# Scores and value sums of four heads per group, B's statistics from one sum, x in halves, and a gate on GpSimd's queue, in a two-layer hybrid trunk

## The chip, the cores and the metric

The kernel runs on one core of a Trainium2 chip. The metric is device time in microseconds (us) of one execution, the median of the runs; lower is better. TensorE (PE) multiplies matrices, VectorE (DVE), ScalarE (ACT) and GpSimd (POOL) work on tiles, SyncE (SP) issues most of the transfers. "Product" below means one matmul instruction.

## The reference, cut to what matters

Two layers over 256 tokens of width 2048, all in float32:

```
for l in range(DEPTH):
    h = rms_norm(x, norm_w[l])
    p = h @ w_in[l]                                   # 2048 x 6668
    oa = sliding_window_sink_attention(qa, ka, va, sinks[l]) * silu(za)   # A: 12 heads of 64, window 128
    ob = conformer_conv_module(ub, ...) * silu(zb)    # B: conv over 31 steps, layer norm, 512 x 512
    oc = rms_norm(gated_deltanet(...)) * silu(zc)     # C: 6 heads of 128, delta rule in chunks
    x = x + concatenate([oa, ob, oc]) @ w_out[l]      # 2048 x 2048
```

In A the scores of a head are a product of 64 rows by 128 queries and 128 or 256 keys; after the softmax the weights are transposed and multiplied with the values of 64 columns. In B the mean and the variance over 512 channels (four tiles of 128 channels) are sums over partitions, made on PE with a matrix of 1/512.

## The kernel before, in words

**Precision.** The large products run with both operands split into a high and a low part (`wh`, `wl` of the weights, the two halves of `xhl` of the activations): high by high, high by low, low by high, three products for one. The small products of A, B and C are plain float32.

**The stream of weights.** `Stream.load` has SP bring the weights in stages of up to 1 MB into `st` (three buffers). `Stream.cuts` cuts a stage into granules of 1024 columns in all: ACT rounds a granule to `wh`, then DVE subtracts to get `wl` (three buffers of each). `token_block` multiplies a block of 512 or 268 columns with the activations stationary; `channel_block` takes 256 columns with the weights stationary. The blocks stand in the list `ORDER`; the first is 512 columns of A's queries (`qk`, 96 products of 512 columns).

**The start.** `load_x` brings x in pieces `xc`; `first_x(i)` transposes 256 columns of it on PE (`xtp`, four transposes), DVE copies the result to `xt`, `set_x` makes `xhl` from it (ACT the high part, DVE the low part), `keep_x` writes `xt` to a scratch tensor `xscr` in memory, from which the residual is read back near the layer's end. `squares` sums the squares of x on ACT; from these come `msq`, on POOL `rstd`, and on PE the row `rowp` of the norm's scale, without which no block's sum can be scaled and leave its PSUM bank. `late_loads` has POOL issue 18 transfers of small parameters (`crow`, `alog`, `prow`, `snk`, `posi`, ...). The masks (`mean_b`, `ucum`, `amask`) come from POOL too.

**A.** `pair(pr)` takes two heads: four products `sc` into two banks, the softmax on DVE and ACT, six transposes `ptp`, six products `ov`. At most two pairs are under way at a time (`"pair": 2`).

**B.** `mixer_b` runs 30 taps of the convolution on DVE and ACT; then `mu` (two products), the squares, `bss` (four products), the row `rowp` of 1/std, the scaled and activated `bs`, which `channel_block` multiplies with the pointwise weights (`PWAT = 4`: after four blocks of the output projection).

**The order.** Tasks are Python generators. Every operation is noted by a `Meter` and put out by `Pace`, which holds for each engine a time from which it is free, with costs written into `price`, and always puts out the operation that by these costs can start first; the trunk's large products go ahead of the tasks unless a task's operation fits in. What comes out is one fixed list for each engine, and each engine works through its list in order. So an operation that is noted later but waits for nothing is put ahead of one noted earlier that waits:

```
for key, l in self.open.items():
    if l:
        free, m = self.at[key], margin if key == "P" else 0.0
        t = max(free, min(n.ready for n in l) + m)
        if t < at or t == at and not best:
            best, at = min((n for n in l if n.ready + m <= t), key=lambda n: n.task.rank), t
```

All instructions are recorded under one line (L346, the call in `Pace.emit`), so rows of the profile are told apart by their tiles.

Of the kernel before, what the change touches and what calls it, by code (L numbers as in the profile page):

```python
# [17 lines left out]
P = 128  # L18
# [409 lines left out]
def hybrid_trunk(ctx: ExitStack, tc: tile.TileContext, x, positions, norm_w, w_in, q_norm_w,  # L428
# [56 lines left out]
    xv = x[0].rearrange("(t p) c -> p t c", p=P)  # L485
    xcs, xat, cols_left = [], [], {}

    def load_x(*cols):

        j = len(xat) // 2  # L490
        if len(xcs) == j:
            xcs.append(big([P, 2, 512], "xc"))
# [27 lines left out]
    posi = const.tile([P, 2], I32, name="posi")  # L520
    crow = [big([DEPTH * KC, 9 * P], "crow") for _ in range(2)]
    pace.free["big"] -= 2

    def late_loads():
        cw = c_conv_w.rearrange("l k c -> (l k) c")
# [104 lines left out]
    ready = []  # L630

# [36 lines left out]
    class Stream:  # L668
# [45 lines left out]
        def cuts(self):  # L714
# [3 lines left out]
            for i, (si, kk, cc, end) in enumerate(self.granules):  # L718
# [7 lines left out]
                S.activation(hi, v, AF.Copy)  # L726
                V.tensor_tensor(lo, v, hi.bitcast(F32), ALU.subtract)
# [52 lines left out]
    def token_block(n, step, act):  # L780
        accs = accs_of(2)
        for k0 in range(0, KT, step):
            hi, lo = stream.next()
            for k in range(step):
                a = act(k0 + k)
                for tb in range(2):
                    ts = slice(tb * P, (tb + 1) * P)
                    acc = accs[tb][:, :n]
                    f, e = k0 + k == 0, k0 + k == KT - 1
                    PE.matmul(acc, a[:, 0, ts], hi[:, k, :], start=f, stop=False)  # L790
                    PE.matmul(acc, a[:, 0, ts], lo[:, k, :], start=False, stop=False)
                    PE.matmul(acc, a[:, 1, ts], hi[:, k, :], start=False, stop=e)
        return accs
# [22 lines left out]
    def keep_x(l, i, xt):  # L816

        (G if l else Q).dma_start(xscr[i], xt.rearrange("p a t -> p (a t)"))
# [10 lines left out]
    def squares():  # L829

        for j in range(4):
            yield lambda: len(xat) > 2 * j + 1
            for tb in range(2):
                sq = mid([P, 512], "sq")
                S.activation(sq, xcs[j][:, tb], AF.Square, accum_out=ssx[:, tb, j:j + 1])
# [411 lines left out]
    def mixer_b(l, h, res):  # L1247
# [51 lines left out]
        V.tensor_tensor(sq[:, 0:2, :], sq[:, 0:2, :], sq[:, 2:4, :], ALU.add)  # L1299
        yield 1  # L1300
        ps = bank([P, 2], "bss")
        for tb in range(2):
            for c in range(2):
                PE.matmul(ps[:, tb:tb + 1], sq[:, c, tb * P:(tb + 1) * P], mean_b[:, 0:1],
                          start=(c == 0), stop=(c == 1))
# [372 lines left out]
    def a_first(l, stt, res):  # L1678
# [61 lines left out]
        def pair(pr):  # L1740
            yield {"mx": 2, "pair": 1}
            pss = [bank([P, 384], "sc") for _ in range(2)]
            for cols, to in ((slice(0, P), slice(0, P)), (slice(P, T), slice(P, 384))):
                for r in range(2):
                    rs = slice(64 * r, 64 * r + 64)
                    PE.matmul(pss[r][:, to], qT[rs, pr, cols], kT[rs, (2 * pr + r) // 3, 0:cols.stop],
                              start=True, stop=True)
            yield
            s2 = []
            for r in range(2):  # L1750
                h = 2 * pr + r
                ps = pss[r]
                s = mp.tile([P, 384], F32, tag="as", bufs=4, name=nm("sm"))
                sk = snk[:, l, h:h + 1]
                V.tensor_tensor_reduce(s[:, 0:P], ps[:, 0:P], amask[:, 1, :], 1.0, sk, ALU.add,
                                       ALU.max, mx[:, h, 0:1])
                V.tensor_tensor_reduce(s[:, P:], ps[:, P:], am, 1.0, sk, ALU.add, ALU.max,
                                       mx[:, h, 1:2])
                s2.append(s)
            drop(2)  # L1760
            hs = slice(2 * pr, 2 * pr + 2)
            V.tensor_scalar(nm_[:, hs, :], mx[:, hs, :], -1.0, None, ALU.mult)
            V.tensor_tensor(ex[:, hs, :], nm_[:, hs, :],
                            snk[:, l, hs].unsqueeze(2).to_broadcast([P, 2, 2]), ALU.add)
            yield
            S.activation(ex[:, hs, :], ex[:, hs, :], AF.Exp)
            for r in range(2):
                h = 2 * pr + r
                for b, seg in ((0, slice(0, P)), (1, slice(P, 384))):
                    S.activation(s2[r][:, seg], s2[r][:, seg], AF.Exp, bias=nm_[:, h, b:b + 1],  # L1770
                                 accum_out=den[:, h, b:b + 1])
            yield
            V.tensor_tensor(den[:, hs, :], den[:, hs, :], ex[:, hs, :], ALU.add)
            V.reciprocal(den[:, hs, :], den[:, hs, :])
            yield
            for r in range(2):
                h = 2 * pr + r
                for b, seg in ((0, slice(0, P)), (1, slice(P, 384))):
# [102 lines left out]
```

## Time and profile before

| | |
|---|---|
| median of 3 runs | 910.84 us (910.77 to 911.11) |
| profiled execution | 913.37 us, its span 911.7 us |
| PE busy | 897.4 us of the span |
| DVE, ACT, POOL busy | 727.9, 567.3, 74.2 us |
| granted TensorE clock | 1.00 throughout |

The span runs from the first to the last instruction of the profiled execution. An engine is busy while one of its instructions is under way; products overlap, so the time that a product costs is read from the start of one to the start of the next. In a row of the timeline, the brackets give the idle time ahead of it and what ended it.

### The profile page before, as it was taken

What the parts mean: (1) busy time and instruction counts of PE and PEld (TensorE: products, weight loads), DVE (VectorE), ACT (ScalarE), POOL (GpSimd) and SP (SyncE); (2) the same over time, 40 slices, a digit from 0 to 9 for tenths busy, and PEclk for the clock granted to TensorE, in tenths of its full rate; (3) what the DMA queues carried; (4) which work ended last, traced back from release to release, by engine and by line L of the source; (5) the groups of instructions that cost most, each with busy time, mean ns of one, the idle gap of its engine ahead of it and who ended that gap; (6) DMA issues with size and microseconds to landing.
All of it is one profiled execution on the core that took longest, in us unless ns stands there. A gap on an engine that the chain in (4) does not pass through costs nothing.

```text
span 911.7 us, 15429 instructions
## 1 busy us (share of the span) xinstructions
PE 897.4 (98%) x5856; PEld 791.8 (87%) x5856; DVE 727.9 (80%) x1405; ACT 567.3 (62%) x1092; POOL 74.2 (8%) x93
## 2 busy tenths in 40 slices
PE   6999999999999999999999999999999999999998
PEld 5899888887789888999888988888788988899998
DVE  5855778999999999657765577699999999985553
ACT  5647845668867665546544596457687676645542
POOL 5000032021001000000000000501200010000000
PEclk9999999999999999999999999999999999999999
DMA  9866467544343655757766554865525435665681
GB/s 301 265 190 185 156 191 195 174 127 134 95 155 96 185 185 161 235 196 264 236 200 192 185 186 148 219 185 153 150 60 167 135 115 186 192 216 184 200 271 36
DMA packets 146186, 161.92 MB, mean 178 GB/s; under 512 B 8191, under 2 KB 129649, under 8 KB 146112
## 3 DMA queue, kind: packets, MB, share of 16 engines
q1 hardware_dynamic: 143808, 155.40, 54.0%
q0 software_dynamic: 2256, 5.52, 2.6%
q8 instruction: 46, 0.75, 0.4%
q14 instruction: 28, 0.23, 0.1%
q10 hardware_dynamic: 48, 0.02, 0.0%
HBM read 152.67 MB, written 8.26 MB: 177 GB/s over the span
## 4 chain that ended last, share of the span: by engine, by line
PE 73%; DVE 13%; issue 5%; DMA 4%; ACT 3%; POOL 1%; SPq 0%; DVEq 0%; POOLq 0%; ACTq 0%
PE acc L346 65%; DVE wl L346 4%; DVE bacc L346 4%; DVE z L346 2%; PE ov L346 1%; DMA xc<-in_x_dram 1%; ACT junk L346 1%; DMA sub<-scry 1%; PE gram L346 1%; PE tsum L346 1%; PE sc L346 1%; DMA scrm<-sub 1%; DMA ms<-scrm 1%; PE ptp L346 1%; ACT wh L346 1%
## 5 line engine op out<-in xcount | busy, mean ns | idle before, releaser
L346 PE MATMUL acc<-xhl,wh 128*128 128x512 f32 x1344 | 476.4, 395 | 0.0
L346 DVE TENSOR_TENSOR wl<-st,wh 128x1024 fp32r<-128x1024 f32 (+1 forms) x276 | 337.8, 1224 | 132.1 <-ACT wh L346 129.3
L346 ACT ACTIVATE wh<-st 128x1024 fp32r<-128x1024 f32 (+1 forms) x276 | 292.3, 1059 | 219.4 <-PE acc L346 194.8
L346 PE MATMUL acc<-xhl,wl 128*128 128x256 f32 x1344 | 382.9, 285 | 0.0
L346 PEld LDWEIGHTS acc<-xhl,wh 128*128 128x128 f32 x1344 | 252.8, 188 | 55.4 <-issue 2.7
L346 PEld LDWEIGHTS acc<-xhl,wl 128*128 128x128 f32 x1344 | 253.4, 189 | 5.6 <-issue 4.7
L346 PE MATMUL acc<-wh,xhl 128*128 128x512 f32 (+1 forms) x384 | 108.0, 365 | 2.7 <-ACT wh L346 2.7
L346 PEld LDWEIGHTS acc<-wh,xhl 128*128 128x128 f32 x384 | 68.6, 191 | 13.7 <-ACT wh L346 3.1
L346 PE MATMUL acc<-wl,xhl 128*128 128x512 f32 (+1 forms) x192 | 69.7, 363 | 0.5 <-DVE wl L346 0.5
L346 DVE SCALAR_TENSOR_TENSOR bacc<-bh,cbt,bacc 128x254 f32<-128x254 f32 (+19 forms) x160 | 68.3, 462 | 0.1
L346 PE MATMUL acc<-yc,wh 128*128 128x256 f32 (+1 forms) x300 | 65.7, 305 | 0.0
L346 PE MATMUL acc<-ya,wh 128*128 128x256 f32 (+1 forms) x300 | 65.5, 305 | 0.0
L346 PE MATMUL acc<-yc,wl 128*128 128x256 f32 x180 | 50.9, 283 | 0.0
L346 PE MATMUL acc<-ya,wl 128*128 128x256 f32 x180 | 50.6, 281 | 0.0
L346 PEld LDWEIGHTS acc<-ya,wh 128*128 128x128 f32 x300 | 48.2, 188 | 2.5
L346 PEld LDWEIGHTS acc<-yc,wh 128*128 128x128 f32 x300 | 48.2, 188 | 2.4
L346 DVE SCALAR_TENSOR_TENSOR ca<-z,cct,ca 128x255 f32<-128x255 f32 (+2 forms) x108 | 47.9, 499 | 2.2 <-ACT ca L346 2.1
L346 ACT ACTIVATE bpr<-bh,cbt 128x255 f32<-128x255 f32 (+9 forms) x80 | 37.6, 488 | 10.1 <-DVE bacc L346 10.0
L346 PE MATMUL acc<-yb,wh 128*128 128x256 f32 (+1 forms) x200 | 43.2, 305 | 0.0
L346 PEld LDWEIGHTS acc<-wl,xhl 128*128 128x128 f32 x192 | 36.6, 191 | 6.4 <-DVE wl L346 1.0
L346 PEld LDWEIGHTS acc<-ya,wl 128*128 128x128 f32 x180 | 34.1, 190 | 0.0
L346 PEld LDWEIGHTS acc<-yc,wl 128*128 128x128 f32 x180 | 34.0, 189 | 0.1
(305 smaller groups left out, 1118.1 us busy)
## 6 DMA issues: line engine op xcount, KB each, us to landing
st<-in_w_in_dram SPq DMA_DIRECT2D x102, 1024.0 KB, 5.3
st<-in_w_out_dram SPq DMA_DIRECT2D x16, 768.0 KB, 5.0
st<-in_w_out_dram SPq DMA_DIRECT2D x10, 1024.0 KB, 5.7
st<-in_w_out_dram SPq DMA_DIRECT2D x12, 512.0 KB, 3.8
st<-in_w_out_dram SPq DMA_DIRECT2D x16, 256.0 KB, 5.6
st<-in_w_in_dram SPq DMA_DIRECT2D x4, 512.0 KB, 8.9
xscr<-xt SPq DMA_DIRECT2D x8, 256.0 KB, 8.7
xt<-xscr SPq DMA_DIRECT2D x8, 256.0 KB, 5.1
```

What stands on the lines that cost most here:

```text
L346: n.f(*n.a, **n.k)
```

## The change

Five things. Two pairs of heads become one task `pairs(p0)`: eight `sc` products into four banks, and twelve `ov` products into one bank with one copy; the two pairs go through the softmax one behind the other. B's two sums over channels get one more addition on DVE, and one product each where there were two. x is loaded and laid out in halves of 256 columns, `set_x` reads the transposes from PSUM and the copy `xt` is made behind it, and the first granule of weights is cut in two pieces. `token_block` multiplies with `wh` first, for both halves of the tokens, and with `wl` last. And a copy on POOL, `gate`, reads the tenth tile of `xhl`; `late_loads` and the layer's first `keep_x` begin when that copy has been noted, and the writes to `xscr` go out from POOL instead of SP.

```diff
-    xv = x[0].rearrange("(t p) c -> p t c", p=P)
+    xv = x[0].rearrange("(t p) (h c) -> p h t c", p=P, c=256)
...
-            a = 256 * (len(xat) % 2)
-            Q.dma_start(xcs[j][:, :, a:a + c], xv[:, :, 512 * j + a:512 * j + a + c])
-            xat.extend(c // 256 * [True])
+            for _ in range(c // 256):
+                h = len(xat) % 2
+                Q.dma_start(xcs[j][:, h], xv[:, 2 * j + h])
+                xat.append(True)
...
+    def hold():
+
+        yield lambda: (0, GATE) in xhl
+        G.tensor_copy(gate, xhl[0, GATE][:, 0, 0:1].bitcast(F32))
+        ready.append("gate")
+        yield "G"
+
     def late_loads():
+        yield lambda: "gate" in ready
...
-                S.activation(hi, v, AF.Copy)
-                V.tensor_tensor(lo, v, hi.bitcast(F32), ALU.subtract)
+                for a in range(0, k, k if i else 1):
+                    b = k if i else a + 1
+                    S.activation(hi[:, a:b], v[:, a:b], AF.Copy)
+                    V.tensor_tensor(lo[:, a:b], v[:, a:b], hi[:, a:b].bitcast(F32), ALU.subtract)
...
-                for tb in range(2):
-                    ts = slice(tb * P, (tb + 1) * P)
-                    acc = accs[tb][:, :n]
-                    f, e = k0 + k == 0, k0 + k == KT - 1
-                    PE.matmul(acc, a[:, 0, ts], hi[:, k, :], start=f, stop=False)
-                    PE.matmul(acc, a[:, 0, ts], lo[:, k, :], start=False, stop=False)
-                    PE.matmul(acc, a[:, 1, ts], hi[:, k, :], start=False, stop=e)
+                f, e = k0 + k == 0, k0 + k == KT - 1
+                for w, part in ((hi, 0), (hi, 1), (lo, 0)):
+                    for tb in range(2):
+                        PE.matmul(accs[tb][:, :n], a[:, part, tb * P:(tb + 1) * P], w[:, k, :],
+                                  start=f and w is hi and not part, stop=e and w is lo)
...
-        (G if l else Q).dma_start(xscr[i], xt.rearrange("p a t -> p (a t)"))
+        G.dma_start(xscr[i], xt.rearrange("p a t -> p (a t)"))
...
         V.tensor_tensor(s2, acc[:, 0:2, :], acc[:, 2:4, :], ALU.add)
+        V.tensor_tensor(s2[:, 0], s2[:, 0], s2[:, 1], ALU.add)
         yield 1
         mu = bank([P, T], "mu")
-        for c in range(2):
-            PE.matmul(mu, mean_b, s2[:, c, :], start=(c == 0), stop=(c == 1))
+        PE.matmul(mu, mean_b, s2[:, 0], start=True, stop=True)
...
-        def pair(pr):
-            yield {"mx": 2, "pair": 1}
-            pss = [bank([P, 384], "sc") for _ in range(2)]
...
+        def pairs(p0):
+
+            both = (p0, p0 + 1)
+            yield {"mx": 4, "pair": 2}
+            pss = [bank([P, 384], "sc") for _ in range(4)]
...
+            op = bank([P, 2, T], "ov")
+            for pr in both:
                 for j in range(3):
-                    PE.transpose(ps[:, j, :], s2[r][:, j * P:(j + 1) * P], ident)
...
+                    for r in range(2):
+                        PE.matmul(op[64 * r:64 * r + 64, pr - p0, P * (j > 0):P * (j > 0) + P],
+                                  va[:, j // 2, (2 * pr + r) // 3, :],
+                                  s2[2 * (pr - p0) + r][:, P * j:P * j + P], start=(j < 2), stop=(j != 1))
...
-        V.tensor_copy(xt, ps)
-        drop()
-        done_x(i // 2)
-        yield
-        yield from set_x(0, i, xt)
+        done_x(i // 2)
+        yield from set_x(0, i, ps)
+        V.tensor_copy(xt, ps)
+        drop()
+        yield
...
         def rest():
+            yield lambda: "gate" in ready
             keep_x(0, i, xt)
```

On POOL, at the start of the program, the changed kernel's list reads as follows (`crow` to `snk` are parameters, `xscr<-xt` the first writes of x).

```order
L346 MEMSET expo 128x64 x2
L346 DMA crow_100<-in_c_conv_w_dram 8x1152
L346 DMA crow_101<-in_c_conv_w_dram 8x1152
L346 DMA alog<-in_c_a_log_dram 128x12
...
L346 DMA prow<-in_k_norm_w_dram 2x48 x2
L346 DMA snk<-in_sinks_dram 128x24
L346 COPY gate<-xhl_256 128x1
L346 DMA posi<-in_positions_dram 128x2x1
L346 DMA xscr<-xt_18_141 128x512
L346 DMA xscr<-xt_28_174 128x512
```

The gate's copy stands behind 17 of the 18 parameter transfers, in the places that they had before; behind it come `posi`, the eight writes of x (before on SP), the masks, and then `rstd`.

On PE, at the start of the program, the changed kernel's list begins so (`acc` are the two sums of the first block, `xtp` sets of four transposes of x).

```order
L346 MATMUL xtp_115<-ident,xc_77 128x128 x4
L346 MATMUL acc_122<-wh_119,xhl_142 128x512
L346 MATMUL acc_123<-wh_119,xhl_142 128x512
L346 MATMUL acc_122<-wh_119,xhl_142 128x512
L346 MATMUL acc_123<-wh_119,xhl_142 128x512
L346 MATMUL xtp_118<-ident,xc_77 128x128 x4
L346 MATMUL acc_122<-wl_120,xhl_142 128x512
L346 MATMUL acc_123<-wl_120,xhl_142 128x512
```

Before, a product with `wl` was the second of the block, and the first five products were followed by twelve transposes at once; now four products with `wh` come first, and the sets of transposes stand between products one or two at a time.

On PE, in A of the first layer, two heads' value sums and the next scores stood like this before (`acc` are products of the input projection).

```order
L346 MATMUL ov_2618<-sm_2378,va_835 64x128
L346 MATMUL acc_2461<-xhl_214,wl_2395 128x256
L346 MATMUL acc_2460<-xhl_270,wh_2462 128x512
L346 MATMUL acc_2460<-xhl_270,wl_2463 128x256
L346 MATMUL acc_2460<-xhl_271,wh_2462 128x512
L346 MATMUL ov_2618<-sm_2379,va_835 64x128
L346 MATMUL ov_2618<-sm_2378,va_835 64x128
L346 MATMUL ov_2618<-sm_2379,va_835 64x128
L346 MATMUL ov_2618<-sm_2378,va_835 64x128
L346 MATMUL ov_2618<-sm_2379,va_835 64x128
```

In the changed kernel four heads' value sums stand like this (`cz` are products of C).

```order
L346 MATMUL ov_2944<-sm_2454,va_842 64x128
L346 MATMUL ov_2944<-sm_2453,va_842 64x128
L346 MATMUL ov_2944<-sm_2454,va_842 64x128
L346 MATMUL ov_2944<-sm_2563,va_842 64x128
L346 MATMUL cz_2923<-cvr_2440,mt_2218 128x128
L346 MATMUL ov_2944<-sm_2564,va_842 64x128
L346 MATMUL ov_2944<-sm_2563,va_842 64x128
L346 MATMUL ov_2944<-sm_2564,va_842 64x128
L346 MATMUL ov_2944<-sm_2563,va_842 64x128
L346 MATMUL ov_2944<-sm_2564,va_842 64x128
```

A pair's six `ov` products were broken one to five by other products, in 11 of the 12 pairs of both layers; now the twelve of four heads are broken once, seven to five, in all six groups. The scores of both layers stood in 15 runs and now stand in 9.

## Rows read from the trace of the kernel before

**Rows 1.** The page, parts 1 and 2: PE's busy time and its clock.

```profile
PE 897.4 (98%) x5856; PEld 791.8 (87%) x5856; DVE 727.9 (80%) x1405; ACT 567.3 (62%) x1092; POOL 74.2 (8%) x93
...
PEclk9999999999999999999999999999999999999999
```

**Rows 2.** Timeline of all engines at the start: start, length, engine, instruction, count.

```profile
5.03 0.69 DVE L346 COPY xt<-xtp 128x512 f32<-128x512 f32 x1 [0.97 <-PE xtp L346]
...
6.57 1.04 ACT L346 ACTIVATE wh<-st 128x1024 fp32r<-128x1024 f32 x1
...
7.66 0.80 PE L346 MATMUL acc<-wh,xhl 128*128 128x512 f32 x1 [2.67 <-ACT wh L346]
...
12.19 2.82 PE L346 MATMUL xtp<-ident,xc 128*128 128x128 f32 x12 [1.20 <-DMA xc<-in_x_dram]
...
15.67 0.63 PE L346 MATMUL acc<-wl,xhl 128*128 128x512 f32 x1
...
16.09 1.05 PE L346 MATMUL acc<-wh,xhl 128*128 128x512 f32 x2
...
17.23 0.63 PE L346 MATMUL acc<-wh,xhl 128*128 128x512 f32 x2
...
18.39 0.40 PE L346 MATMUL acc<-wl,xhl 128*128 128x512 f32 x1
```

**Rows 3.** Stretches at the start: engines' busy time, clock, DMA share, GB/s.

```profile
0.00:5.00 5.00, 1.40 (x5) 0.89 (x5) 0.36 (x2) 1.28 (x1) 4.33 (x15) 1.00 0.56 182
5.00:10.00 5.00, 1.88 (x4) 1.19 (x5) 3.04 (x5) 2.91 (x4) 2.60 (x6) 1.00 1.04 229
10.00:15.00 5.00, 3.80 (x16) 3.08 (x15) 1.84 (x3) 2.11 (x7) 2.72 (x6) 1.00 1.05 364
```

**Rows 4.** Timeline of POOL: its first transfers, and the norm's power.

```profile
1.65 1.25 POOL L346 DMA_DIRECT2D crow<-in_c_conv_w_dram  x2
...
31.09 0.98 POOL L346 TENSOR_TENSOR rstd<-msq,expo 128x2 f32<-128x2 f32 x1 [12.23 <-DVE msq L346]
```

**Rows 5.** Issues that touch xscr: ns min/median/max, first and last start in us.

```profile
L346 SPq DMA_DIRECT2D xscr<-xt x8: 319/658/2007, 10.9 to 28.6; - x8
...
L346 POOL DMA_DIRECT2D xscr<-xt x4: 540/546/609, 418.9 to 464.0; - x4
```

**Rows 6.** Timeline of PE around one pair's value sums in layer 0.

```profile
255.81 0.40 PE L346 MATMUL acc<-xhl,wh 128*128 128x512 f32 x1
256.13 0.43 PE L346 MATMUL ov<-sm,va 128*64 128x128 f32 x2
256.50 0.38 PE L346 MATMUL acc<-xhl,wl 128*128 128x256 f32 x1
256.72 0.39 PE L346 MATMUL acc<-xhl,wh 128*128 128x512 f32 x1
257.04 0.87 PE L346 MATMUL ov<-sm,va 128*64 128x128 f32 x10
257.84 0.38 PE L346 MATMUL acc<-xhl,wl 128*128 128x256 f32 x1
```

**Rows 7.** Timeline of PE around one pair's scores in layer 0.

```profile
242.03 0.93 PE L346 MATMUL sc<-akT,aqT 64*128 64x128 f32 x8
242.88 0.38 PE L346 MATMUL acc<-xhl,wl 128*128 128x256 f32 x1
```

**Rows 8.** Timeline of PE around B's statistics in layer 0.

```profile
361.38 1.10 PE L346 MATMUL mu<-s,mean_b 128*128 128x256 f32 x4 [0.91 <-DVE s L346]
362.13 0.47 PE L346 MATMUL acc<-xhl,wl 128*128 128x256 f32 x1
...
366.40 0.95 PE L346 MATMUL bss<-mean_b,bsq 128*128 128x1 f32 x8
```

**Rows 9.** Timeline of DVE and PE around B's pointwise products in layer 0.

```profile
383.05 0.69 DVE L346 TENSOR_TENSOR bs<-bacc,bs 128x512 fp32r<-128x512 f32 x1
...
400.65 0.40 PE L346 MATMUL acc<-bs,wh 128*128 128x256 f32 x2
```

More of the change, by code (lines that the diff above doesn't have):

```diff
@@ L1302, in mixer_b @@
         for tb in range(2):
-            for c in range(2):
-                PE.matmul(ps[:, tb:tb + 1], sq[:, c, tb * P:(tb + 1) * P], mean_b[:, 0:1],
-                          start=(c == 0), stop=(c == 1))
+            PE.matmul(ps[:, tb:tb + 1], sq[:, 0, tb * P:(tb + 1) * P], mean_b[:, 0:1],
+                      start=True, stop=True)
         yield
@@ L1738, in a_first @@
         left = [HA // 2]
-        def pair(pr):
-            yield {"mx": 2, "pair": 1}
-            pss = [bank([P, 384], "sc") for _ in range(2)]
[L1743 to L1747, printed above, removed]
+        def pairs(p0):
[3 more added lines that the diff above has]
+            for pr in both:
+                for cols, to in ((slice(0, P), slice(0, P)), (slice(P, T), slice(P, 384))):
+                    for r in range(2):
+                        rs = slice(64 * r, 64 * r + 64)
+                        PE.matmul(pss[2 * (pr - p0) + r][:, to], qT[rs, pr, cols],
+                                  kT[rs, (2 * pr + r) // 3, 0:cols.stop], start=True, stop=True)
@@ L1748, in pair @@
             yield
             s2 = []
[L1750 to L1764, printed above, removed]
-            yield
[L1766 to L1771, printed above, removed]
@@ new lines, in pairs @@
+            for pr in both:
+                hs = slice(2 * pr, 2 * pr + 2)
+                S.activation(ex[:, hs, :], ex[:, hs, :], AF.Exp)
+                for r in range(2):
+                    h = 2 * pr + r
+                    for b, seg in ((0, slice(0, P)), (1, slice(P, 384))):
+                        S.activation(s2[h - 2 * p0][:, seg], s2[h - 2 * p0][:, seg], AF.Exp,
+                                     bias=nm_[:, h, b:b + 1], accum_out=den[:, h, b:b + 1])
+                yield
@@ new lines, in pairs @@
+            for pr in both:
+                hs = slice(2 * pr, 2 * pr + 2)
+                V.tensor_tensor(den[:, hs, :], den[:, hs, :], ex[:, hs, :], ALU.add)
+                V.reciprocal(den[:, hs, :], den[:, hs, :])
+                yield
+                for r in range(2):
+                    h = 2 * pr + r
+                    for b, seg in ((0, slice(0, P)), (1, slice(P, 384))):
+                        V.tensor_scalar(s2[h - 2 * p0][:, seg], s2[h - 2 * p0][:, seg],
+                                        den[:, h, b:b + 1], None, ALU.mult)
+                yield 2
+                pss = []
+                for r in range(2):
+                    ps = bank([P, 3, P], "ptp")
+                    pss.append(ps)
+                    for j in range(3):
+                        PE.transpose(ps[:, j, :], s2[2 * (pr - p0) + r][:, j * P:(j + 1) * P], ident)
+                yield
+                for r in range(2):
+                    S.activation(s2[2 * (pr - p0) + r], pss[r].rearrange("p j q -> p (j q)"), AF.Copy)
+                drop(2)
@@ new lines, in pairs @@
+            yield 1
+            op = bank([P, 2, T], "ov")
+            for pr in both:
+                for j in range(3):
+                    for r in range(2):
+                        PE.matmul(op[64 * r:64 * r + 64, pr - p0, P * (j > 0):P * (j > 0) + P],
+                                  va[:, j // 2, (2 * pr + r) // 3, :],
+                                  s2[2 * (pr - p0) + r][:, P * j:P * j + P], start=(j < 2), stop=(j != 1))
+            yield
+            S.activation(o[:, p0:p0 + 2, :], op, AF.Copy)
@@ L1800, in pair @@
             drop()
-            drop(1, "pair")
-            left[0] -= 1
+            drop(2, "pair")
+            left[0] -= 2
             if not left[0]:
@@ L1805, in pair @@
                 drop(2, "big")
-        for pr in range(HA // 2):
-            pace.add(1, pair(pr))
+        for p0 in range(0, HA // 2, 2):
+            pace.add(1, pairs(p0))
     ORDER = [('qk', 0), ('u', 0), ('v', 0), ('va', 0), ('ck', 0), ('ck', 1), ('ck', 2), ('qk', 1), ('cq', 0), ('cq', 1), ('cq', 2), ('u', 1), ('v', 1), ('cv', 0), ('cv', 1), ('cv', 2), ('zc', 0), ('zc', 1), ('zc', 2), ('za', 0), ('za', 1), ('za', 2), ('zb', 0), ('zb', 1)]
@@ L1848, in hybrid_trunk @@
     pace.add(-1, stream.cuts())
+    pace.add(1, hold())
     pace.add(1, late_loads())
```

66 lines of the change are left out of this document (29 added, 37 removed).

## The prediction

> **What bounds the kernel now.** I read the page first. PE is busy for 897.4 of the 911.7 us of the span, and its clock row stands at the top digit in all slices [rows 1]. So time can be won in only two ways: by filling the few places where PE has nothing to do, or by giving PE less to do. A busy PE is not a PE at its peak, so next I read the starts of its products. From 17.23 to 18.39 lie five products of 512 columns, 0.23 us each; just before, from 15.67 to 16.09, one takes 0.42 [rows 2]. 512 columns in 0.42 us is the 1.2 GHz level, in 0.23 us the 2.4 GHz level; the page's clock row reads 1.00 in both, so only the starts tell them apart. Of PE's idle 14.3 us, 7.9 lie in the first 15 us, where it is busy for 7.08 [rows 1, 3]; over the other 897 us 6.4 are left. At the start PE waits 2.67 us until 7.66 for ACT's first rounding of weights, and 1.20 us until 12.19 for x [rows 2]. What it does until then runs at the half pace. Why x comes late is seen in the stretches: from 5 to 10 us the DMA engines are full (share 1.04) and yet move only 229 GB/s, against 364 in the next 5 us at the same share [rows 3]. That is while GpSimd's small transfers, issued from 1.65 us on [rows 4], are under way.
>
> The last view is PE around the small products of A. A product of another shape costs more than its columns, and this is paid at each change to and fro [rows 6, 7].
>
> **The change, part by part.**
>
> *The start.* The first product needs `xhl` and `wh`. Now `set_x` reads PSUM, so the DVE copy of 0.69 us no longer stands ahead of it, and the first rounding is of 512 columns instead of 1024, half of 1.04 us [rows 2]. That is 1.2 us: the first product at about 6.4 instead of 7.66. Four products with `wh` follow, where before the second one already waited for `wl`. At 0.43 us each they last to 8.2. Then PE's list has the second set of transposes. Its half of x is complete when 1.05 MB have passed in SP's order; by rows 3, 0.91 MB have passed at 5 us and 2.06 MB at 10 us, so 5.6 us. The x of 12.19 was the end of the first 1.84 MB, which had passed at about 9, so landing lags by up to 3 us: 7.6 to 8.6. So this wait is short. Eight products and the third set (x of the same 12.2 us as before) come next, then twelve products, the fourth set, and four more products by 17. The next x (3.67 MB; 14.4 us by the same count, landing near 17.2 to 17.9) lets sets five and six end at 18.4.
>
> So at 18.4 PE has done 28 products and six sets of transposes. Before it had done 16 products and four sets. Twelve products at 0.23 are 2.8 us, two sets at full pace some 0.45 us each (an estimate: twelve transposes took 2.82 us at half pace [rows 2]), 3.7 in all. I take off 0.4 for short waits for x on a list that was fixed beforehand: **3.3 us**. This has PE at full pace from about 12 us, since its work is nearly unbroken from 6.4 on; before, it was at half pace through broken work and rose at 17 after unbroken work from 12.19 [rows 2]. If the pace rose no earlier than 17 us again, the same 28 products and six sets would end at 20.1, and the gain be 1.6 us. The Trainium skill, "TensorE: Matmul & The Clock Gate" (Part 1: The HAM clock gate), has the slow state as the default, which activity lifts; by that the earlier work is also the earlier full pace, and the sum is the one with 3.3. Bounds of this part: 0.3 (x and weights bind as before) to 5 (no wait at all: the 2.67 and 1.20 us and the half pace of some six products).
>
> *The transfers held back.* They are not. The gate's copy stands behind 17 of the 18 in POOL's list, and an engine works through its list in order, so `crow` goes out at 1.65 us as before [rows 4]. I count nothing for this. What is held is `posi` and the eight writes of x. Those leave SP, where one took up to 2.0 us to issue, for POOL, where such a write takes 0.55 [rows 5]. SP's next weights are for the block behind the first one's 96 products (22 us at 0.23), so this gains nothing either. But behind the writes on POOL stand the masks and `rstd`. The gate opens near 20 us (the fifth block of x rounded); `posi` and eight writes at 0.55 to 0.75 take until 26, the masks another 1, `rstd` 0.98 [rows 4]: near 29. In between DVE's casts wait for a mask. PE comes to `rowp` near 31.4. This has about 1 to 2 us of cover, and I count 0.
>
> *A.* Two records of `ov` cost 256.50 - 255.81 - 0.23 = 0.46 us, ten cost 257.84 - 256.72 - 0.23 = 0.89 [rows 6]: four steps of two heads side by side in 0.43, 0.11 a step, and the rest is the change of shape, 0.24 a run. A pair is two and ten: 1.35. Four heads are now fourteen and ten: 0.89 + 2 x 0.11 = 1.11, and 0.89, so 2.00 instead of 2.70. Six groups: 4.2, less 0.4 for the one pair that was not broken before: 3.8. Eight records of `sc` cost 0.85 [rows 7]. The columns alone, two passes of 256 and two of 128, are three passes of 256, at most 0.19 each by `mu` [rows 8]: 0.56, so a run carries 0.29 of change. Six runs fewer: 1.7. Together **5.5 us**. Bounds: 0 if PE now waits in A as long as it saves, 7 if even the breaks left over cost nothing.
>
> What is moved here: the four heads need four free banks at once, and two groups can't overlap. In PE's list the third group's scores of layer 0 now stand 175 large products later than the last pair's before. A's result is not late for that: its first use still stands some 400 products on. The softmax itself has the same instructions.
>
> *B.* One `mu` product of two goes, half of 0.75 us, and two of four `bss` products, half of 0.95 [rows 8]: 0.85 a layer, **1.7 us** for both. DVE gets two additions of 256 columns a layer, some 0.4 us each (0.69 for 512 [rows 2]). They lie on the way to `bs`, and that way is shorter now: with A's work on DVE later, B's taps end later. In layer 0, 245 products of 256 columns stood between `rowp` and the first product with `bs` on PE, now 110. Before, the last `bs` was done at 383.74 and first used at 400.65, 16.9 us on [rows 9]. 135 products at 0.12 are 15.9 us. So 1.0 us of cover is left. I count 0; where the cover is gone, each us that DVE is late is one us of PE. Ahead of `mu` PE waited 0.91 us for DVE [rows 8]; the new addition could make it 1.3, which is left to the range.
>
> *The order in `token_block`* has the same number of products and weight loads; only the start uses it.
>
> The sum is 3.3 + 5.5 + 1.7 = 10.5 us. The profiled execution took 913.37, 1.7 more than its span; it would take 902.9. The median is 2.5 below the profiled one, and the same sum gives 910.84 - 10.5 = **900.3 us**.
>
> **The rivals.**
>
> *The start is bound by transfers (0.12).* For it: the DMA share is 1.04 and more from 5 us on [rows 3], and the small transfers still take their part. Against: PE is left with work between the arrivals. The start then gives 0.3: 903.3.
>
> *New waits in A or B (0.08).* For it: 1.0 us of cover before `bs`, and a list in which PE waits behind the seventh `ov` if the fourth head's copy is late. One granule of 24 products late is 2.8 us; one or two of them, 903 to 906. Against: `bs` needs the same four granules from `rowp` on as before.
>
> *The transfers are held back after all (0.03).* It would bring the rate of 5 to 10 us from 229 to 364 GB/s, 1.85 us [rows 3]: 898.4. Against: POOL's list.
>
> *Slower (0.05): POOL's writes stop the norm.* If a write of x took POOL as long as the longest took SP, 2.0 us [rows 5], the eight would end at 37 instead of 26, `rstd` near 39 and `rowp` near 40.5. PE's list is in order, so 9 us of work behind `rowp` would stand: about 909. From 2.2 us a write it is slower than before. Against: 0.55 on POOL for the same write in the second layer's part.
>
> **How the numbers follow.** My forecast has 0.72, its own range 897.5 to 903. The range from 896.5 (start 5, A 7, B 1.7 give 897.1, with the clock and waits a little better) to 905.5 takes in the first rival and most of the second, and leaves out the slow case. About 0.2% (1.8 us) is what a measurement of this kernel tells from no change. Faster 0.93; same 0.02 and slower 0.05 come from the last rival and the tail of the second.
>
> **What the profile after would show.** The first product near 6.4 us, full pace by 13, `rowp` near 31. `crow` issued at 1.65 as before; if it comes after 15 us, I am wrong on the gate. `ov` in runs of fourteen and ten, 2.0 us for four heads; `mu` x2 and `bss` x4 a layer. No idle PE before `bs` in layer 0; a gap there is the second rival, a gap at `rowp` the slower one. I would be wrong by most if the list of PE, fixed with costs of the planner, met softmax results that come later on the chip.

## The result, and the profile after

The changed kernel takes 899.54 us (898.39 to 903.32, four runs) against 910.98 before (910.77 to 911.99): a ratio of 0.9879, 95% interval 0.9849 to 0.9910, faster by 11.4 us. The profiled execution is the slowest of the four, 903.32 with a span of 901.6; the other spans are 896.7 to 898.2. A later series gave 0.9851 (0.9836 to 0.9865), 14.1 us. The prediction was 900.3.

The page of the profiled execution, parts 1, 2 and 4, against [rows 1]:

```profile
PE 889.4 (99%) x5844; PEld 792.1 (88%) x5844; DVE 729.6 (81%) x1410; ACT 565.6 (63%) x1087; POOL 81.5 (9%) x102
...
PEclk9999999999999999999999999999989999999999
...
PE 88%; DVE 7%; issue 2%; DMA 2%; ACT 0%; POOL 0%; SPq 0%; DVEq 0%; POOLq 0%; ACTq 0%
```

PE is busy 8.0 us less, and one digit of the clock row is an 8, of which more below. Timeline of PE at the start, and the stretches (PE, PEld, DVE, ACT, POOL, clock, DMA share, GB/s), against [rows 2, 3]:

```profile
7.38 2.08 PE L346 MATMUL acc<-wh,xhl 128*128 128x512 f32 x4 [2.06 <-ACT wh L346]
9.26 1.05 PE L346 MATMUL xtp<-ident,xc 128*128 128x128 f32 x4
9.96 1.20 PE L346 MATMUL acc<-wl,xhl 128*128 128x512 f32 x2
10.96 1.42 PE L346 MATMUL acc<-wh,xhl 128*128 128x512 f32 x4
```

```profile
5.00:10.00 5.00, 2.94 (x11) 2.12 (x9) 2.67 (x5) 3.98 (x9) 2.81 (x6) 1.00 1.00 226
10.00:15.00 5.00, 5.00 (x25) 4.14 (x24) 3.41 (x7) 4.01 (x10) 3.50 (x7) 1.00 1.07 356
```

The first product is only 0.28 us earlier, but from there PE hardly stops: 5.00 of 5.00 us from 10 to 15, where it was 3.80. By 18.23 us PE has started 28 products and six sets of transposes. The first channel block starts at 38.15 us instead of 41.19. Timeline of POOL, against [rows 4, 5]:

```profile
1.66 1.25 POOL L346 DMA_DIRECT2D crow<-in_c_conv_w_dram  x2
...
18.98 0.38 POOL L346 COPY gate<-xhl 128x1 f32<-128x1 f32 x1 [4.41 <-ACT xhl L346]
...
20.03 3.24 POOL L346 DMA_DIRECT2D xscr<-xt  x6
...
29.48 0.79 POOL L346 TENSOR_TENSOR rstd<-msq,expo 128x2 f32<-128x2 f32 x1 [0.28 <-DVE msq L346]
```

`crow` still goes out at 1.66; the gate's copy holds `posi` and the writes of x alone, and `rstd` comes at 29.48. Timeline of PE around value sums of layer 1 and B's statistics of layer 0, against [rows 6, 8]:

```profile
730.75 0.82 PE L346 MATMUL ov<-sm,va 128*64 128x128 f32 x10
731.50 0.39 PE L346 MATMUL acc<-xhl,wl 128*128 128x256 f32 x1
731.82 0.87 PE L346 MATMUL ov<-sm,va 128*64 128x128 f32 x10
732.62 0.50 PE L346 MATMUL acc<-xhl,wh 128*128 128x512 f32 x1
...
368.73 0.67 PE L346 MATMUL mu<-s,mean_b 128*128 128x256 f32 x2 [1.04 <-DVE s L346]
...
374.44 0.50 PE L346 MATMUL bss<-mean_b,bsq 128*128 128x1 f32 x4
```

(The first row is the end of a run of fourteen records that began at 730.48; one value sum is two records.) Fourteen records take 1.02 from first start to the next product, ten 0.80.

**Where the time went.** The time from one record's start to the next was summed by group over the two stretches with A, B and C (from the first channel product behind the layer's third token block to the first product with `bs`, layer 0 and 1 together); what a large product takes beyond its usual 0.23 or 0.12 us counts for the group behind it, so waits are included. In us:

```
kernel                      A's stage starts  ov     sc     ptp   mu,bss  other small  large   both stretches
before                          138.62       16.58  12.58   7.50   5.41     46.62     432.64     521.23
changed (e0_after)              135.80       11.67  10.89   6.63   3.06     45.51     432.02     510.00
start alone (e1_start)          135.98       16.40  13.26   7.96   5.62     45.30     433.35     522.01
A alone (e2_a)                  138.86       12.13   9.66   6.85   5.26     47.54     432.60     514.05
B alone (e3_b)                  137.63       16.58  12.58   7.51   3.88     46.43     432.43     519.63
six runs of ov (e5_ov)          135.68        9.12  12.17   6.60   3.99     45.10     431.80     509.13
ov by pairs (e6_ovpair)         135.16       10.23  11.30   6.64   3.35     47.83     432.16     511.29
token order (e8_tokorder)       136.67       12.13   9.66   7.60   3.45     47.10     430.85     510.80
ptp reversed (e10_trans)        135.50       11.58  10.43   9.62   3.30     46.03     431.99     512.82
```

Second row against first: 2.8 us are won by the start and 11.2 in the two stretches: `ov` 4.9, `sc` 1.7, `mu` and `bss` 2.4, the softmax's transposes 0.9, other small products 1.1, the rest large products standing closer. The row of e2_a holds some 2 us of a stretch at half clock in layer 1 (below).

**The lost 4 us of the profiled execution** lie in layer 1. Stretches of after, then of the same kernel in the later series:

```profile
650.00:655.00 5.00, 5.00 (x88) 3.58 (x88) 4.64 (x12) 3.58 (x9) 0.00 (x0) 1.00 0.67 212
655.00:660.00 5.00, 4.25 (x62) 3.36 (x63) 4.31 (x13) 4.39 (x9) 0.00 (x0) 0.68 0.03 5
660.00:665.00 5.00, 5.00 (x21) 4.25 (x20) 2.85 (x6) 1.33 (x3) 0.00 (x0) 0.64 0.00 0
```

```profile
655.00:660.00 5.00, 5.00 (x75) 4.12 (x76) 4.78 (x14) 4.86 (x11) 0.00 (x0) 1.00 0.04 14
660.00:665.00 5.00, 5.00 (x45) 4.34 (x44) 4.96 (x11) 3.54 (x7) 0.00 (x0) 1.00 0.05 7
```

The granted clock is 0.68 and 0.64 where it is 1.00 in the other execution; there a product of 512 columns takes 0.42 us to the next start, the 1.2 GHz level. By the sums of the table, made for this execution too, `sc` takes 2.2 us more than in the other, and the large products 2.0.

### The profile page after: what moved, and what is told of

Same layout as the page of the kernel before. It is cut to its first block, busy times and chain, and to the rows that moved or that the text cites. A ratio compares the mean times of both kernels' runs of the same rounds, so it can differ in the third digit from the quotient of the medians.

```text
span 901.6 us, 15432 instructions
## 1 busy us (share of the span) xinstructions
PE 889.4 (99%) x5844; PEld 792.1 (88%) x5844; DVE 729.6 (81%) x1410; ACT 565.6 (63%) x1087; POOL 81.5 (9%) x102
## 4 chain that ended last, share of the span: by engine, by line
PE 88%; DVE 7%; issue 2%; DMA 2%; ACT 0%; POOL 0%; SPq 0%; DVEq 0%; POOLq 0%; ACTq 0%
PE acc L346 77%; DVE wl L346 3%; DVE bacc L346 3%; PE gram L346 2%; PE sc L346 1%; PE ov L346 1%; DVE z L346 1%; PE co L346 1%; PE tsum L346 1%; PE ptp L346 1%; PE cz L346 1%; DMA xt<-xscr 1%; DMA st<-in_w_in_dram 1%; PE dec L346 0%; DMA th<-xscr 0%
## 5 line engine op out<-in xcount | busy, mean ns | idle before, releaser
L346 ACT ACTIVATE wh<-st 128x1024 fp32r<-128x1024 f32 (+2 forms) x277 | 292.7, 1057 | 238.5 <-PE acc L346 209.3
L346 DVE TENSOR_TENSOR wl<-st,wh 128x1024 fp32r<-128x1024 f32 (+2 forms) x277 | 338.0, 1221 | 121.9 <-ACT wh L346 120.7
L346 PE MATMUL acc<-wh,xhl 128*128 128x512 f32 (+1 forms) x384 | 93.5, 363 | 2.1 <-ACT wh L346 2.1
L346 PEld LDWEIGHTS acc<-wh,xhl 128*128 128x128 f32 x384 | 66.2, 191 | 13.3 <-ACT wh L346 2.5
L346 PE MATMUL acc<-wl,xhl 128*128 128x512 f32 (+1 forms) x192 | 54.5, 364 | 0.0
L346 PEld LDWEIGHTS acc<-wl,xhl 128*128 128x128 f32 x192 | 33.9, 190 | 5.0 <-DVE wl L346 0.2
L346 DVE TENSOR_TENSOR z<-acc,z 128x256 f32<-128x256 f32 x76 | 31.8, 429 | 5.1 <-ACT z L346 5.1
```

The costliest lines, as they stand in the source:

```text
L346: n.f(*n.a, **n.k)
```

## The experiments

Each series ran on one chip beside the kernel before (medians 912.72, 911.94 and 913.01 in the three), so kernels of different series are compared by their ratios.

**e0_after**: the changed kernel itself.

> The changed kernel once more, to see how often its time has the 4 us that one stretch at half clock took in the profiled execution (656.8 to 663.6 us). Theory 1, the drop belongs to this order of the products and comes in some executions: about one run in four near 902 to 903 us with a mean granted clock of 0.996, the others 898 to 900 us with 0.999 or 1. Theory 2, the drop was a chance of that one execution and no matter of the kernel: all runs 898 to 900 us.

898.64 us, four runs from 898.01 to 899.14, clock 1.0 in all. So the half-clock stretch is no fixed part of the kernel; between the two theories this alone doesn't decide.

**e1_start, e2_a, e3_b**: the three parts one by one. In the first, `pair` and B as before; in the second, `pairs` alone; in the third, these two lines with their single products:

```diff
+        V.tensor_tensor(s2[:, 0], s2[:, 0], s2[:, 1], ALU.add)
...
+        V.tensor_tensor(sq[:, 0], sq[:, 0], sq[:, 1], ALU.add)
```

> The start edits alone (x in halves, the order of the token blocks, the cuts of the first weights, the transfers at the gate), with scores, value sums and B's statistics as before. Theory 1, the parts add: the start term as measured in the changed kernel, 3.0 us, so 907.9 us against 910.9, with the first channel block near 38.2 us after the span's start and no later gain. Theory 2, part of what layer 0 gave later (9.8 us by its end) also comes from the start, since x's late transfers and GpSimd's writes move: 904 to 906 us.

> Scores and value sums of four heads in one group alone, all else as before. Theory 1, the prediction's term: 5.5 us, so 905.4. Theory 2, the term was too small, because with four heads the transposes and the other small products of this stage also interrupt the large products less often: 9 to 10 us, so 901 to 902 where the granted clock stays at 1; with the stretch at half clock, 905 to 906 and a row at 0.64 in layer 1. If no run here has that stretch, the drop needs more than the grouping.

> B's statistics from one sum alone, all else as before. Theory 1, the prediction's term: 1.7 us less in all, so 909.2. Theory 2, the extra additions on VectorE stand on the path (the wait ahead of mu grew from 1.08 to 1.20 us in layer 0): 0.3 to 0.6 us of it are lost, 909.7. Theory 3, the wait hides the whole of it, since products that fill the wait now stand elsewhere: 910.9, no change.

Start 911.27, ratio 0.9986 (0.9977 to 0.9996), 1.5 us; A 904.78, 0.9914 (0.9898 to 0.9930), 7.9 us; B 910.83, 0.9983 (0.9974 to 0.9992), 1.9 us. The start does win its 2.7 us up to the first channel block (38.46), but a start that ends earlier meets the tasks of A and C at other places, and the fixed list comes out differently: scores (now in 16 runs instead of 15) and transposes take 0.7 and 0.5 us more over the two stretches. Neither theory of e1_start had a loss there. A's 7.9 lies between the two theories (5.5 and 9 to 10); its profiled execution, 906.83, has a stretch at half clock too, the other four are 903.03 to 905.16. B's is the first; in its profile 1.6 us show in the two stretches. A's stage also starts 1.0 us earlier there without any edit (137.63), which is the scatter of the start. The three sum to 11.3 where the whole gave 14.1. The intervals (0.9 to 1.5 us to either side) may hold part of the 2.8; the table shows that the columns don't add up either (`mu` and `bss` give 1.5 alone and 2.4 in the whole, since the wait ahead of `mu` in layer 1 shrank too). How much is order and how much scatter stays open.

**e4_held**: `ready` is set only after the copy has been put out, so that all of POOL's transfers wait for it.

```diff
         G.tensor_copy(gate, xhl[0, GATE][:, 0, 0:1].bitcast(F32))
-        ready.append("gate")
         yield "G"
+        ready.append("gate")
```

> The changed kernel with GpSimd's seventeen parameter transfers really behind its gate copy (about 19 us into the span), where the changed kernel issues crow at 1.66 us. Theory 1, the stretch 5 to 10 us is slow for x and the first weights because GpSimd's small pieces share the transfer engines (226 to 229 GB/s there, 356 after it): it moves over 300 GB/s, the first product stands near 6.4 us instead of 7.1 to 7.4, the first channel block 0.7 to 1.9 us earlier, time 896.7 to 898. Theory 2, those transfers are not what slows the stretch: first product as before, 898.6. Theory 3, what is held back is then missed by a consumer: a new wait of PE in the first 45 us, over 899.

899.26 us, ratio 0.9853: no change. The stretch and the first product (e4_held), then what comes later:

```profile
5.00:10.00 5.00, 3.14 (x12) 2.25 (x10) 2.67 (x5) 3.96 (x9) 0.00 (x0) 1.00 1.04 357
```

```profile
4.32 1.11 PE L346 MATMUL xtp<-ident,xc 128*128 128x128 f32 x4
...
7.29 0.80 PE L346 MATMUL acc<-wh,xhl 128*128 128x512 f32 x1 [1.86 <-ACT wh L346]
...
38.93 1.29 PE L346 MATMUL pt<-ident,crow 8*128 8x8 f32 x18
```

The first half of theory 1 is right, 357 GB/s instead of 208 to 226; its second half is not. The first product comes no earlier. The first channel block does start at 36.49 us, but only because 1.7 us of the parameters' transposes have moved behind its start: A's stage starts at 136.14, against 135.80. What sets the first product is seen on ACT, in the kernel before and here:

```profile
1.29 1.28 ACT L346 ACT_TABLE_LOAD   x1 [1.29 <-PEq L1867]
5.75 0.91 ACT L346 ACTIVATE xhl<-xt,prm 128x256 fp32r<-128x256 f32 x2 [3.18 <-DVE xt L346]
```

```profile
4.58 1.28 ACT L346 ACT_TABLE_LOAD   x1 [4.58 <-DVE prm L346]
5.88 0.84 ACT L346 ACTIVATE xhl<-xtp,prm 128x256 fp32r<-128x256 f32 x2
6.61 1.15 ACT L346 ACTIVATE wh<-st 128x512 fp32r<-128x512 f32 x2
```

ACT's table load of 1.28 us used to lie in idle time at 1.29. Now it stands behind ACT's wait for `prm` and ends at 5.86, directly ahead of the first `xhl`. The four transposes that this `xhl` waits for are done at 5.43, so the load costs the start some 0.4 us, and faster transfers of x and weights don't get past it. (`prm` comes from the transfer `prow`, which PE awaited until 3.99 here and 3.89 in the changed kernel.) In all eleven profiles of the new start the load begins between 4.11 and 4.58 us.

**e7_nogate**: no gate, layer 0's writes of x on SP again (`(G if l else Q).dma_start(...)`). **e9_cut**: the first weights rounded in one piece.

```diff
-                for a in range(0, k, k if i else 1):
-                    b = k if i else a + 1
...
+                S.activation(hi, v, AF.Copy)
+                V.tensor_tensor(lo, v, hi.bitcast(F32), ALU.subtract)
```

> The changed kernel without the gate, with layer 0's writes of x on SP's queue again. Theory 1, the prediction: gate and queue of these writes are worth nothing, since SP's next weights are not yet wanted: 898.6 within 0.6, first channel block near 38.2 us. Theory 2, a write on SP (up to 2.0 us to issue) stands ahead of halves of x and of first weights: PE waits for x or weights between 15 and 30 us, first channel block 39 us or later, 899.5 to 901.

> The changed kernel with the first weights rounded in one piece of 1024 columns on ScalarE and VectorE, as before. Theory 1, the first rounding sets the first product: 0.5 us later (1.04 us against about 0.58 for half), and the whole start is late by it: 899.1, first channel block 38.7. Theory 2, the arrivals of x set the pace of the start: the 0.5 us is made up at the next wait for x, 898.6.

899.52 (0.9854) and 898.87 (0.9848): neither edit changes the time measurably. Without the gate the first channel block starts at 37.45 us, with the whole cut at 37.86. There the first product is at 7.56, but the transposes behind it stand at 9.01, no later than in the changed kernel.

**e8_tokorder**: a token block's products in the order of before.

```diff
-                for w, part in ((hi, 0), (hi, 1), (lo, 0)):
-                    for tb in range(2):
...
+                for tb in range(2):
...
+                    PE.matmul(acc, a[:, 0, ts], hi[:, k, :], start=f, stop=False)
+                    PE.matmul(acc, a[:, 0, ts], lo[:, k, :], start=False, stop=False)
+                    PE.matmul(acc, a[:, 1, ts], hi[:, k, :], start=False, stop=e)
```

> The changed kernel with the products of a token block in the order of before (one half of the tokens after the other, each with high, low, high part). Theory 1, the prediction: this order is worth nothing by itself, 898.6 within 0.6. Theory 2, it is what lets four products run before the low part of the first weights is there: a wait of 0.4 to 0.5 us for wl returns at the first products, 899.1, and nothing later. Theory 3, any change early in the program also moves the scheduler's order in both layers by more than that (here 13 runs of value sums and 7 of scores instead of 12 and 9): the start as in theory 1 or 2, but the two layers' attention stages off by 1 to 2 us in either direction.

900.25, 0.9872 (0.9858 to 0.9887): by the ratios 1.9 us slower than the changed kernel. Its start:

```profile
6.86 0.80 PE L346 MATMUL acc<-wh,xhl 128*128 128x512 f32 x1 [1.85 <-ACT wh L346]
8.45 0.80 PE L346 MATMUL acc<-wl,xhl 128*128 128x512 f32 x1 [0.79 <-DVE wl L346]
```

The wait for `wl` is back with 0.79 us, and the first channel block starts at 39.24, against 37.45 to 38.56 in the nine other profiles with this start (e4_held apart): theory 2, at about 1 us, though from one profile, 0.7 us above the highest of the nine. Then theory 3: the scheduler's list for A becomes that of e2_a (`ov` and `sc` stand at 12.13 and 9.66 in both), and 0.8 us more is lost in the two stretches, where 1 to 2 were expected.

**e5_ov, e6_ovpair**: how the value sums stand.

```diff
-            for pr in both:
+            for pr in both[::-1]:
                 for j in range(3):
-                    for r in range(2):
+                    for r in (1, 0):
```

```diff
+            for pr in both:
+                yield 1
+                op = bank([P, T], "ov")
...
+                S.activation(o[:, pr, :], op, AF.Copy)
```

> The changed kernel with the value sums of four heads issued in the reverse order of heads, which leaves each group of twelve products in one piece: six runs of value sums in the program, where the changed kernel has twelve (7 and 5) and the kernel before has 23. Theory 1, what counts is how often value sums interrupt the large products: from 23 to 13 runs the grouping alone gave 4.4 us in two layers, 0.44 us a run, so six runs fewer give 2.6 us more: 896.0. Theory 2, the first product of the run of five waited for its head's copy, and the wait only moves ahead of the whole group: 898 to 899, with a wait of PE on ACT ahead of each group.

> The changed kernel with the value sums of each pair of heads in a bank and with a copy of their own, as in the kernel before; scores stay grouped by four. The scheduler then sets them in twelve runs of six, as many runs as in the changed kernel (twelve of 7 and 5), where the kernel before had 23. Theory 1, the number of runs sets the time: no change against the changed kernel, 898.6 within 0.6. Theory 2, four heads in one bank and one copy are themselves the gain (fewer banks, fewer instructions on ScalarE): half to all of the 4.4 us of the value sums is lost, 901 to 903.

898.45 (0.9849) and 900.47 (0.9872). In e5_ov a group is one piece (251.33 to 252.79), and `ov` gives the 2.55 us that theory 1 counted; in e6_ovpair a pair is:

```profile
251.33 1.53 PE L346 MATMUL ov<-sm,va 128*64 128x128 f32 x24
252.79 0.50 PE L346 MATMUL acc<-xhl,wh 128*128 128x512 f32 x1
```

```profile
287.73 0.88 PE L346 MATMUL ov<-sm,va 128*64 128x128 f32 x12
288.54 0.38 PE L346 MATMUL acc<-xhl,wl 128*128 128x256 f32 x1
```

The time of theory 1 (896.0) did not come; that of theory 2 (898 to 899) did, but without the wait on ACT that was its reason. By the table the gain went to scores (1.3 us) and to `mu` (0.9). The waits of PE after the start (us in all, times, longest) show the one at `mu`, and a new one at `p64p`, though the other small products, among which `p64p` is counted, take 0.4 us less in all:

```profile
PE mu L346 <- DVE s L346: 2.3, 2, 1.1
PE p64p L346 <- issue: 1.2, 2, 0.6
```

(1.4 us at `mu` and none at `p64p` in the changed kernel.) e6_ovpair's value sums cost 10.23, less than the 11.67 of the groups of four, though both stand in twelve runs: six and six products instead of seven and five. Ten records take as long as twelve (731.82 to 732.62 and 287.73 to 288.54). The single records of these traces show why. The records of two heads start 0.007 us apart, side by side, and one such step takes 0.11 us. So two products side by side take two steps, and a product whose partner stands in the other run takes two steps alone. Seven and five are 14 steps; six and six, or twelve in one piece, are 12; one and five for each pair, as in the kernel before, are 16. Twelve steps fewer over the six groups are 1.3 us (an estimate: 12 x 0.11), which is most of the 1.44 that e6_ovpair wins here and half of e5_ov's 2.55. So a bank and a copy for four heads are not the gain; fewer runs are, and runs that leave no product without its partner. The time of e6_ovpair is 1.9 us more all the same, and fits neither theory; its other small products take 2.3 us more (47.83 against 45.51).

**e10_trans, e11_all**: transposes of the softmax reversed as well; then the scores too.

```diff
-                for r in range(2):
-                    ps = bank([P, 3, P], "ptp")
-                    pss.append(ps)
-                    for j in range(3):
+                pss = [bank([P, 3, P], "ptp") for _ in range(2)]
+                for r in (1, 0):
+                    ps = pss[r]
+                    for j in (2, 1, 0):
```

> The changed kernel with value sums in reverse order of heads, as in the run with six runs of value sums, and each pair's six transposes of the softmax in reverse order too. The scheduler then sets the transposes in 12 runs instead of 28 to 30; value sums stand in 11 runs, scores in 9. Theory 1, each run of transposes costs what the lines of before and after show for a change of shape there, 0.09 to 0.13 us: 18 fewer are 1.6 to 2.3 us, 896.3 to 897. Theory 2, as in the run before (value sums 1.2 us a layer less, waits of PE of 1.2 us in their place): what is won in runs comes back as waits ahead of p64p, mu or the transposes: 898 to 899.

> The run before with scores in reverse order as well: 10 runs of scores, 12 of transposes, 10 of value sums, in all 24 fewer changes away from the large products than in the changed kernel. Theory 1, fewer changes, less time: 895.5 to 897. Theory 2, waits take their place: 898 to 899. If it comes out over 899, the order itself costs more than it saves.

902.86 (0.9892) and 900.04 (0.9863): fewer changes and more time. PE's waits of 0.15 us and more from 130 to 850 us come to 5.6 us in e10_trans, against 1.4 in e0_after, which covers its loss; in e11_all they come to 2.6. The longest of e10_trans:

```profile
PE ptp L346 <- DVE sm L346: 2.0, 2, 1.8
PE mu L346 <- DVE s L346: 1.4, 2, 1.2
```

And the runs gave nothing. Six transposes in one piece (e10_trans), then one transpose between large products (after):

```profile
209.18 0.81 PE L346 MATMUL ptp<-ident,sm 128*128 128x128 f32 x6
209.75 0.48 PE L346 MATMUL acc<-xhl,wh 128*128 128x512 f32 x1
210.07 0.28 PE L346 MATMUL acc<-xhl,wl 128*128 128x256 f32 x1
```

```profile
256.25 0.27 PE L346 MATMUL ptp<-ident,sm 128*128 128x128 f32 x1
256.28 0.48 PE L346 MATMUL acc<-xhl,wh 128*128 128x512 f32 x1
256.59 0.38 PE L346 MATMUL ptp<-ident,sm 128*128 128x128 f32 x2
```

210.07 - 209.18 - 0.23 is 0.66 for six, 256.59 - 256.25 - 0.23 is 0.11 for one: 0.11 each, however they stand. Theory 1 was wrong on the price of a break, and theory 2 on the size of the waits.

## Why the prediction was right, and what in it was not

The time and the sign are right, the sum of 10.5 us is too small by 1 to 3.6, and its terms are off in both directions, so that the time came within 1 us of the forecast is partly luck: the median of the later series lies 3.6 us beyond the sum.

**The start, 3.3.** Measured 3.0 at the first channel block (1.5 at the end, alone). The count for 18.4 us held: 28 products and six sets of transposes had been started by 18.23. The step that failed is "the first product at about 6.4", which came at 7.38: the copy of 0.69 us is gone from the path, but the table load came onto it. In the changed kernel the four transposes end at 5.33 and `xhl` starts behind the load at 5.78, so the load costs some 0.4 us. Another 0.35 is `prow`, which happened to land later (PE's `pt` at 3.89 against 3.54), and about 0.1 the first rounding, 0.63 us for half. In the six profiles where `pt` came at 3.52 to 3.59 the first product stands at 6.81 to 6.89. A load in idle time would give about 6.4 there (an estimate from these rows; not tried). That PE hardly waits afterwards was right, and full pace by 13 too. The count used the new order of the token block (four products with `wh` ahead of `wl`) without giving it a price; it carries about 1 us (e8_tokorder). The finer cut, on which 0.5 us of the count rested, brings the first product 0.2 to 0.5 us ahead (7.56 without it, 7.09 and 7.38 with it) and gave nothing further on.

**The transfers held back, 0.** Right: `crow` at 1.66, 17 transfers ahead of the gate, `rstd` at 29.48 against "near 29", `rowp` at 32.10 with 0.5 us of waiting against 31.4. The rival that priced a real hold at 1.85 us was wrong on the price: it is 0 (e4_held).

**A, 5.5.** This is the term that was mis-sized: 7.9 alone. The value sums were counted at 3.8 (15.8 before, 12.0 after) and gave 4.9 in the changed kernel (16.58 and 11.67), 4.5 alone; scores at 1.7, which is what they gave in the changed kernel, and 2.9 alone. The pattern of `ov` was as predicted, fourteen and ten. The count priced a broken pair by [rows 6], 0.46 and 0.89, but in seven of the eleven broken pairs of the kernel before the run of ten costs 1.0; and the new runs often stand next to other small products (212.54 to 214.44: `ov`, `p32p`, `ov`), where the runs of fourteen and ten take 1.02 and 0.80 from start to next start, without the 0.1 to 0.2 us that is added behind a large product. The two lone steps that the split into seven and five costs (0.22 us a group, see e6_ovpair) are in the counted 2.00. Scores stood in fifteen runs before, three pairs being broken, and stand in nine in the changed kernel, six fewer as counted; e2_a has seven. Transposes, which the count left as they were, gave 0.7 to 0.9, in more runs than before (30 against 24).

**B, 1.7.** Right: 1.9 alone. No idle PE ahead of `bs`, as forecast, but the 1.0 us of cover was not there: in the changed kernel the last `bs` is done at 390.98, 0.17 us behind the first product with `bs` at 390.81 (the other three tiles were done by 389.64).

**The rivals.** No new wait in A or B of the size of a granule came with the change itself; it came with e10_trans, at 1.8 us. POOL's writes took 0.54 us each.

## What to carry to other kernels

Price a break in the stream of large products by the shape that breaks it: the products of 64 rows or columns cost by the run, the full 128 by 128 ones by the piece. Where two heads' products go side by side, don't break a run at an odd product. In a kernel whose order is one fixed list, a part's own gain is read from its stretch, and 1 to 3 us of the whole come from where everything else happens to land; variants with fewer breaks were no faster. When a copy is taken off the start's path, look at what the compiler puts ahead of the next engine's first instruction.

## What the runs showed of the hardware

**A charge by the run, for some shapes only.** Value sums (128x64) of four heads took 2.7 to 3.0 us in four runs, 2.1 in two (1.11 and 1.00), 1.55 in one; 128x128 transposes take 0.11 each in any split. Taken apart (an estimate from the table, at 0.11 us a step), a run costs 0.2 us in the changed kernel, e5_ov and e6_ovpair and 0.28 in the kernel before, and the rest is steps. The Trainium skill, "TensorEngine Tiling (Array Packing)" (Key Properties), says that a change of tiling mode drains the engine. The traces agree: the shapes of other size pay some 0.2 us a run or more, and the transposes, which share the large products' mode, pay nothing.

**The clock fell behind a stretch in which PE was at work.** In three of the eleven profiles with grouped heads (after, e2_a, e7_nogate) the granted clock fell in layer 1 in the same part of the program, behind a stretch with many small products of A and C and few large ones; in after this ran from 650 to 656 us, and PE was busy all the while (5.00 of 5.00 us from 650 on). In after and e7_nogate a pause of 0.76 and 0.28 us that the profile puts down to nothing ("issue") comes first: in after PE stops at 656.27, and the granted clock is 1.00 up to 656.80; in e7_nogate PE goes on at 655.82 and the clock falls at 656.2. The same products in the same order ran in e0_after, e4_held and e9_cut with neither pause nor fall, and e10_trans has a pause of 1.79 us (646.76) without a fall. In e2_a there is a wait of 0.5 us for DVE 2 us ahead of the fall, which e8_tokorder has too, without a fall. Timeline of after, its stretches around the fall, and the stretches of e7_nogate and e2_a where it fell:

```profile
650.34 1.09 PE L346 MATMUL ov<-sm,va 128*64 128x128 f32 x14
651.36 0.57 PE L346 MATMUL p32p<-m,kk 32*32 32x32 f32 x24
...
654.91 0.94 PE L346 MATMUL u32p<-p,mt 32*32 32x32 f32 x46
655.78 0.49 PE L346 MATMUL sc<-akT,aqT 64*128 64x128 f32 x3
657.02 2.50 PE L346 MATMUL sc<-akT,aqT 64*128 64x256 f32 x11 [0.76 <-issue]
```

```profile
656.30:656.80 0.50, 0.00 (x0) 0.00 (x0) 0.50 (x2) 0.48 (x2) 0.00 (x0) 1.00 0.00 0
656.80:657.00 0.20, 0.00 (x0) 0.00 (x0) 0.20 (x2) 0.18 (x1) 0.00 (x0) 0.52 0.00 0
```

```profile
655.00:660.00 5.00, 4.72 (x29) 3.60 (x24) 4.96 (x13) 4.33 (x9) 0.00 (x0) 0.66 0.01 3
```

```profile
660.00:665.00 5.00, 4.48 (x60) 3.65 (x60) 4.97 (x14) 4.85 (x12) 0.00 (x0) 0.76 0.02 3
```

The Trainium skill, "TensorE: Matmul & The Clock Gate" (Part 1: The HAM clock gate), has the slow state follow idleness; here PE was busy, with products of 32 and 64 rows or columns, until 0.5 us ahead of the fall in after and up to it in the other two. The three profiles without grouped heads (before, e1_start, e3_b) show no such stretch, nor do the other eight with them. Three in eleven against none in three is too few to call the grouping its cause. The other 34 runs of these kernels have mean clocks of 0.999 or 1.000, where the three with a fall have 0.996 to 0.998. So the cause stays open, as does why it comes in some executions only.
